# Half of the attention's q and k turned on VectorE and through memory instead of on TensorE

## The chip, the cores and the metric

The kernel runs on one core of one Trainium2 chip. Its time is device microseconds (us) for one execution. Five engines work side by side, each on its own queue of instructions: TensorE (PE) multiplies matrices into PSUM, VectorE (DVE) and ScalarE (ACT) do the element work, GpSimd (POOL) and SyncE (SP) mostly start transfers; ScalarE can start them too. They meet at semaphores.

## The reference

One layer of a bidirectional encoder, 512 tokens (8 rows of 64) by 1024 features:

```python
x = x + 0.5 * swiglu1(rmsnorm(x))
h = rmsnorm(x); xr, gr, q, k, v, ga, gb = split(h @ w_in)
y_lru = (rglru_fwd(conv(xr)) + rglru_bwd(conv(xr))) * gelu(gr)
q = rmsnorm_per_head(q, q_norm) * 64**-0.5;  k = rmsnorm_per_head(k, k_norm)
y_att = softmax(q k^T + relative_bias, 8 x 16 window) v      # 16 heads of 64
x = x + (sigmoid(ga) * y_lru + sigmoid(gb) * y_att) @ w_out
x = x + 0.5 * swiglu2(rmsnorm(x))
```

All is float32. A scale that only depends on the position within a head (`q_norm`, `k_norm`) sits on both sides of the product q k^T.

## The kernel before

Precise products are made from split operands: a weight tile `wraw` that was loaded by SP is cast to a rounded high part `wh` (line 138, ScalarE; in the gate chunks with odd f line 140, VectorE) and a low part `wl` = raw − high (line 141, VectorE), and each product is three matmuls (lines 166 to 168). There are four buffers each for `wh` and `wl` and three for `wraw`, used in turn: the cast for one chunk can begin when the matmuls that read the chunk four places before it have ended.

The stages follow each other on TensorE: FFN 1, the xr projection with the recurrent branch, the q, k and v projections for features 0 to 511 and then 512 to 1023 ("half 0" and "half 1", `hf`), then 24 gate chunks of 24 matmuls with 512 columns each (chunk 0 to 23 below: eight for `gr`, eight for `ga`, eight for `gb`), w_out and FFN 2. The work of the attention and of the recurrence is written as Python generators, `lanes`, from which `weave` takes a step at fixed rates (`RATE`) in the middle and at the end of each chunk; `hold` keeps an instruction behind the last chunk matmul recorded so far. From this the Tile framework's scheduler makes one fixed order for each engine.

`heads(hf)` is the attention of one half, in four groups `fi` of two heads. First q and k (tokens on the partitions, tiles `qk`) are multiplied by their norms `rq` (line 1004). Then, per group, `start(fi)` turns four 128 x 128 blocks of q and four of k on TensorE (lines 1013 and 1015, into PSUM), and splits them: `qh` and `kh` by ScalarE (1019, 1022), `ql` and `kl` by VectorE (1021, 1024). `scores(fi)` multiplies them (line 1045, the first matmul reads `kl` and `qh`), VectorE adds the bias table `bm` (1065), ScalarE takes the exponentials (1072, eight of them with an accumulator read each), VectorE scales the rows (1077). `ship` turns the weights in 32 x 32 blocks (1086, 1087), sends them to memory by SP and back by POOL as `PT`; `apply` (1108) multiplies with v, two groups later in half 1, and ScalarE copies the result out as `att` (1118). In half 1 `start(fi + 1)` follows `scores(fi)` in the program.

Between these, the gates are evicted by VectorE (1173), activated by ScalarE (1177) and multiplied into `A` (1187, 1190).

Of the kernel before, what the change touches and what calls it, by code (L numbers as in the profile page):

```python
# [16 lines left out]
P = 128  # L17
# [63 lines left out]
    "t1": {"att": 0.75, "tail": 0.75, "lru": 2},  # L81
    "g": {"att": 0.7, "tail": 0.7, "lru": 1.5, "v": 0.5},
# [4 lines left out]
def block_kernel(ctx: ExitStack, tc, a, out):  # L87
# [19 lines left out]
    NBIG = 42  # L107
# [553 lines left out]
    lanes = {"att": [], "tail": [], "lru": [], "v": []}  # L661
    due = {"att": 0.0, "tail": 0.0, "lru": 0.0, "v": 0.0}
# [113 lines left out]
    gk = small[:, C_KN : C_KN + 1]  # L776
# [27 lines left out]
    def lru():  # L804
# [52 lines left out]
        def use(f, d):  # L857
            r, ix = got[f, d]
            hold(nc.vector.tensor_tensor(ix, ix, xc[f], ALU.mult))
            th = big_t(n="th")  # L860
# [72 lines left out]
    def qk_raw(w, hf, st):  # L933
# [6 lines left out]
        for j, t in enumerate(raws):  # L940
            sq = big_t(n="sq")
# [41 lines left out]
    def bias(g):  # L983

        for hp in range(2):
            bms[g, hp] = tiny.tile([P, 640], F32, tag="bm", bufs=4, name=nm("bm"))
            ld = nc.gpsimd.dma_start(bms[g, hp], a["rpb"][g * 2 + hp])
            if g == 0:
                after(ld, mark["xr"])

    def heads(hf, raws, st):
# [9 lines left out]
        for w in range(2):  # L1001
            for j in range(NCB):
                t = raws[w][j].rearrange("p (h d) -> p h d", d=HD)
                hold(nc.vector.tensor_tensor(t, t, rq[:, w, j, :].unsqueeze(2).to_broadcast([P, 8, HD]), ALU.mult))
            yield
        qk, rss, soft, PTs = {}, {}, {}, {}


        def start(fi):
            fs = slice(fi * P, (fi + 1) * P)  # L1010
            pq, pk = aux_t(), aux_t()
            for j in range(NCB):
                hold(nc.tensor.transpose(pq[:, j * P : (j + 1) * P], raws[0][j][:, fs], ident))
            for j in range(NCB):
                hold(nc.tensor.transpose(perm(pk)[:, j], raws[1][j][:, fs], ident))
            rev = lambda t: t.rearrange("p (j t) -> p j t", j=NCB)[:, :, ::-1]
            fwd = lambda t: t.rearrange("p (j t) -> p j t", j=NCB)
            qh, ql, kh, kl = (big_t(F32R, n=n) for n in ("qh", "ql", "kh", "kl"))
            nc.scalar.activation(rev(qh), fwd(pq), AF.Copy, scale=gq8)
            with tc.high_priority():  # L1020
                nc.vector.scalar_tensor_tensor(rev(ql), fwd(pq), gq8, rev(qh.bitcast(F32)), ALU.mult, ALU.subtract)
            nc.scalar.activation(kh, pk, AF.Copy, scale=gk)
            with tc.high_priority():
                mark["kl"] = nc.vector.scalar_tensor_tensor(kl, pk, gk, kh.bitcast(F32), ALU.mult, ALU.subtract)
# [3 lines left out]
        def scores(fi, n2s):  # L1028
# [22 lines left out]
            for n2, hp in [(n2, hp) for n2 in n2s for hp in range(2)]:  # L1051
# [23 lines left out]
                for i, pt in enumerate(parts):  # L1075
                    n = n2 * 2 + i
                    nc.vector.tensor_scalar(pt, pt, rs[:, hp, n : n + 1], None, ALU.mult)
# [49 lines left out]
        if hf == 1:  # L1127
            yield
        LC = ATT_LAG[hf]
        for i, (fi, n2s) in enumerate(units):  # L1130
# [181 lines left out]
```

## Time and profile before

| what | value |
|---|---|
| median of 3 runs | 1084.0 us (1082.72 to 1085.13) |
| the profiled execution | 1082.5 us, span of its instructions 1080.7 us |
| busy: PE, DVE, ACT, POOL | 1075.3, 770.5, 561.6, 197.8 us |
| attention of half 0 (first turn, last scores) | 495 to 565 us of the span |
| attention of half 1 (first scores, last `apply`) | 598 to 675 us of the span |

The engines overlap, so their busy times don't add up; the span is what one engine's queue, with its waits, takes from the first instruction to the last. In a timeline each row is: start, duration, engine, line, operation, output <- inputs, count, and in brackets the idle time ahead of it and what ended that. In the groups of instructions the numbers are total busy time and mean duration in ns.

### The profile page before, as it was taken

To read this page: it belongs to the slowest core of one execution; us is meant where nothing else is said; L and a number is where in the kernel's file an instruction comes from. 1 tells how busy PE (TensorE), PEld (TensorE's weight loads), DVE (VectorE), ACT (ScalarE), POOL (GpSimd) and SP (SyncE) were. 2 spreads that over 40 slices of the span, in tenths; PEclk is the share of its full clock that TensorE was granted. 3 is DMA by queue.
4 is the path that set the end of the run, shared out by engine and by line. 5 is a ranking of instruction groups with operands and counts; after the bars stand their busy time and mean duration, and the time that the engine had idled before them with its cause. 6 is when DMAs were issued, how large, how long until landed. Compare 5 with 4: busy or idle time off the path is not lost.

```text
span 1080.7 us, 14413 instructions
## 1 busy us (share of the span) xinstructions
PE 1075.3 (99%) x5121; PEld 883.1 (82%) x5121; DVE 770.5 (71%) x1222; ACT 561.6 (52%) x867; POOL 197.8 (18%) x340
## 2 busy tenths in 40 slices
PE   9999999999999999999999999999999999999998
PEld 7888888888888778788877888888888888888887
DVE  7799778774327876999868986758687787764322
ACT  8755555553215778877354642456455555543320
POOL 0110002431000441330345232000001001332000
PEclk9999999999999999999999999999999999999999
DMA  9879675974324685573777576665476777676222
GB/s 356 182 228 246 180 192 135 248 250 148 98 83 146 194 231 155 169 212 104 229 235 219 170 242 205 192 223 160 97 188 188 187 210 167 184 241 198 93 71 79
DMA packets 67464, 198.18 MB, mean 183 GB/s; under 512 B 11072, under 2 KB 12864, under 8 KB 67392
## 3 DMA queue, kind: packets, MB, share of 16 engines
q1 hardware_dynamic: 46736, 136.66, 37.6%
q0 software_dynamic: 20512, 60.34, 25.0%
q8 instruction: 40, 0.66, 0.2%
q14 instruction: 32, 0.26, 0.1%
q10 hardware_dynamic: 144, 0.26, 0.1%
HBM read 162.06 MB, written 26.74 MB: 175 GB/s over the span
## 4 chain that ended last, share of the span: by engine, by line
PE 96%; DVE 2%; DMA 1%; ACT 1%; issue 0%; SPq 0%; ACTq 0%; DVEq 0%
PE acc L318 20%; PE aux L318 15%; PE acc L166 10%; PE acc L168 10%; PE acc L167 10%; PE acc L926 4%; PE acc L927 4%; PE acc L928 4%; PE aux L168 4%; PE aux L166 4%; PE aux L167 4%; PE aux L493 2%; PE aux L1108 1%; PE aux L837 1%; DMA vd<-v 1%; PE aux L1045 1%
## 5 line engine op out<-in xcount | busy, mean ns | idle before, releaser
L141 DVE TENSOR_TENSOR wl<-wraw,wh 128x1024 fp32r<-128x1024 f32 (+2 forms) x147 | 168.9, 1150 | 153.4 <-ACT wh L138 153.0
L138 ACT ACTIVATE wh<-wraw 128x1024 fp32r<-128x1024 f32 (+2 forms) x135 | 134.5, 998 | 224.6 <-PE acc L167 158.2
L141 DVE TENSOR_TENSOR wl<-pair,wh 128x1024 fp32r<-128x1024 f32 x80 | 97.6, 1223 | 42.2 <-ACT wh L138 41.9
L138 ACT ACTIVATE wh<-pair 128x1024 fp32r<-128x1024 f32 x80 | 84.7, 1061 | 77.5 <-PE aux L318 47.8
L166 PE MATMUL acc<-xh,wh 128*128 128x512 f32 x288 | 114.0, 396 | 0.0
L168 PE MATMUL acc<-xh,wl 128*128 128x512 f32 x288 | 112.6, 391 | 0.0
L167 PE MATMUL acc<-xl,wh 128*128 128x512 f32 x288 | 112.5, 391 | 0.0
L318 PE MATMUL aux<-wh,s 128*128 128x512 f32 x320 | 98.5, 389 | 0.0
L318 PE MATMUL acc<-wh,s 128*128 128x512 f32 x320 | 98.5, 389 | 0.0
L926 PE MATMUL acc<-wh,xh 128*128 128x512 f32 x192 | 75.7, 394 | 0.0
L927 PE MATMUL acc<-wh,xl 128*128 128x512 f32 x192 | 74.8, 389 | 0.0
L928 PE MATMUL acc<-wl,xh 128*128 128x512 f32 x192 | 74.7, 389 | 0.0
L318 PEld LDWEIGHTS acc<-wh,s 128*128 128x128 f32 x320 | 60.1, 188 | 12.5
L318 PEld LDWEIGHTS aux<-wh,s 128*128 128x128 f32 x320 | 60.1, 188 | 12.5
L167 PE MATMUL aux<-hl,wh 128*128 128x512 f32 (+1 forms) x179 | 69.3, 387 | 0.0
L168 PE MATMUL aux<-hh,wl 128*128 128x512 f32 (+1 forms) x179 | 69.3, 387 | 0.0
L166 PE MATMUL aux<-hh,wh 128*128 128x512 f32 (+1 forms) x179 | 69.0, 387 | 0.0
L168 PE MATMUL acc<-hh,wl 128*128 128x512 f32 (+1 forms) x176 | 68.1, 387 | 0.0
L167 PE MATMUL acc<-hl,wh 128*128 128x512 f32 (+1 forms) x176 | 68.1, 387 | 0.0
L166 PE MATMUL acc<-hh,wh 128*128 128x512 f32 (+1 forms) x176 | 68.0, 387 | 0.0
L166 PEld LDWEIGHTS acc<-xh,wh 128*128 128x128 f32 x288 | 54.1, 188 | 13.0 <-issue 2.3
L168 PEld LDWEIGHTS acc<-xh,wl 128*128 128x128 f32 x288 | 54.1, 188 | 11.5 <-issue 0.4
(230 smaller groups left out, 2412.3 us busy)
## 6 DMA issues: line engine op xcount, KB each, us to landing
wraw<-wqkv SPq DMA_DIRECT2D x24, 512.0 KB, 4.7
wraw<-wg SPq DMA_DIRECT2D x24, 512.0 KB, 8.0
wraw<-w1d SPq DMA_DIRECT2D x22, 512.0 KB, 3.7
wraw<-w2d SPq DMA_DIRECT2D x22, 512.0 KB, 3.4
PT<-w1s SPq DMA_DIRECT2D x20, 512.0 KB, 7.0
hT<-hd POOLq DMA_DIRECT2D x80, 128.0 KB, 3.9
PT<-w2s SPq DMA_DIRECT2D x20, 512.0 KB, 4.5
hd<-ht SPq DMA_DIRECT2D x32, 256.0 KB, 6.0
```

Source lines behind the costliest of these rows:

```text
L138: mark["H"] = nc.scalar.activation(H, raw, AF.Copy)
L141: mark["L"] = nc.vector.tensor_tensor(L, raw, H.bitcast(F32), ALU.subtract)
L166: nc.tensor.matmul(ps, wh, xh, start=first, stop=False, skip_group_check=skip)
L167: nc.tensor.matmul(ps, wh, xl, start=False, stop=False, skip_group_check=skip)
L168: mark["mm"] = nc.tensor.matmul(ps, wl, xh, start=False, stop=last, skip_group_check=skip)
L318: mark["mm"] = nc.tensor.matmul(pss[tb], x_[:, s], w_[:, c], start=first and k == 0 and x_ is xh_ and w_ is H, stop=k == 3 and w_ is L, sk ...
L493: mark["mm"] = nc.tensor.matmul(pre[tb], x_[:, tb * P : (tb + 1) * P], w_, start=k == 0 and x_ is xh[k] and w_ is H, stop=k == KT - 1 and ...
L837: prev, mm = mm, nc.tensor.matmul(ps[d][b], W[w][o, c], X[x][o], start=x == 1, stop=w + x == 0)
L926: nc.tensor.matmul(pss[j], xh[kk][:, tj], H[:, s], start=kk == 0, stop=False)
L927: nc.tensor.matmul(pss[j], xl[kk][:, tj], H[:, s], start=False, stop=False)
L928: mark["mm"] = nc.tensor.matmul(pss[j], xh[kk][:, tj], L[:, s], start=False, stop=kk == KT - 1)
L1045: mm = hold(nc.tensor.matmul(ps[hp][:, cs], q_[o, n * P : (n + 1) * P], keys(k_[o]), start=k_ is kl, stop=q_ is ql))
```

## The change

- For half 1 the 32 turns on TensorE go. After the norms, VectorE turns each pair of q and k tiles in 32 x 32 blocks (line 1013 of the new kernel) into a `pair` buffer, SP writes it to a new memory tile `qd` (1017, 1023), and `fetch(fi)` reads the blocks of one group back, turned, into `xqk`: four transfers started on ScalarE's queue (1033), 128 KB each, in pieces of 256 bytes. `qh`, `ql`, `kh`, `kl` are made from `xqk` in SBUF (1061 to 1066).
- There is one `xqk` buffer. `fetch(fi + 1)` stands behind the copies that read the group before.
- The norms and turns of half 1 are a lane of their own, `prep`, that runs while half 0's attention does; the first scores of half 1 come two chunks earlier.
- k's norm weight is multiplied into `gq8`, so k is only copied, and `kl` is a plain subtraction.
- In half 1 the rows of the softmax are scaled by ScalarE (1122) instead of VectorE.
- All gate weights are cast by ScalarE: twelve casts leave VectorE.
- The bias tables are loaded ahead of the scores that read the group before, at high priority.
- The pool of 2 KB tiles has 40 buffers instead of 42; the squares of q and k and three `tanh` tiles of the recurrence use other buffers.

```diff
     "t0": {"att": 0.0, "lru": 3.25},
-    "t1": {"att": 0.75, "tail": 0.75, "lru": 2},
-    "g": {"att": 0.7, "tail": 0.7, "lru": 1.5, "v": 0.5},
+    "t1": {"att": 0.75, "tail": 0.75, "lru": 2, "prep": 1.0},
+    "g": {"att": 0.7, "tail": 0.7, "lru": 1.5, "v": 0.5, "prep": 1.0},
 }
 ...
         return f"{s}_{uid[0]}"
-    NBIG = 42
+    NBIG = 40
     def big_t(dt=F32, shape=(P, T), n="b"):
 ...
     after(nc.vector.tensor_scalar(gq8, small[:, C_QN : C_QN + 1], HD**-0.5, None, ALU.mult), mark["h"])
-    gk = small[:, C_KN : C_KN + 1]
+    nc.vector.tensor_tensor(gq8, gq8, small[:, C_KN : C_KN + 1], ALU.mult)
     state = {}
 ...
             hold(nc.vector.tensor_tensor(ix, ix, xc[f], ALU.mult))
-            th = big_t(n="th")
+            if d == 1 and f < 3:
+                th = big.tile([P, T], F32, name=nm("th"), **(dict(tag="xqk", bufs=1) if f == 0 else dict(tag="PT", bufs=5)))
+            else:
+                th = big_t(n="th")
             act("tanh", nc.scalar.activation(th, r, AF.Tanh, scale=sp4[:, f * 2 + d : f * 2 + d + 1]))
 ...
         for j, t in enumerate(raws):
-            sq = big_t(n="sq")
+            sq = big.tile([P, T], F32, tag="pt", bufs=2, name=nm("sq"))
             after(nc.scalar.activation(sq, t, AF.Square), copy)
 ...
             bms[g, hp] = tiny.tile([P, 640], F32, tag="bm", bufs=4, name=nm("bm"))
-            ld = nc.gpsimd.dma_start(bms[g, hp], a["rpb"][g * 2 + hp])
+            with tc.high_priority():
+                ld = nc.gpsimd.dma_start(bms[g, hp], a["rpb"][g * 2 + hp])
             if g == 0:
                 after(ld, mark["xr"])
-    def heads(hf, raws, st):
+    def norm_qk(raws, st, qd):
         rq = tiny.tile([P, 2, NCB, 8], F32, tag="rq", name=nm("rq"))
 ...
         yield
-        for w in range(2):
-            for j in range(NCB):
+        out = []
+        for j in range(NCB):
+            for w in range(2):
                 t = raws[w][j].rearrange("p (h d) -> p h d", d=HD)
                 hold(nc.vector.tensor_tensor(t, t, rq[:, w, j, :].unsqueeze(2).to_broadcast([P, 8, HD]), ALU.mult))
+            if qd is not None:
+                t2 = pair_t().rearrange("p a b -> p (a b)")
+                for w in range(2):
+                    nc.vector.transpose(
+                        t2.rearrange("p (c f w i) -> p w f c i", c=NCB, f=4, w=2)[:, w],
+                        raws[w][j].rearrange("p (f c i) -> p f c i", c=NCB, i=32))
+                while out:
+                    hold(nc.sync.dma_start(*out.pop()))
+                out.append((qd[j], t2))
+                yield
+            elif j % 2 == 1:
+                yield
+        if qd is not None:
+            hold(nc.sync.dma_start(*out.pop()))
             yield
+            yield
+            fetch(qd, 0)
+
+    xs = {}
+
+    def fetch(qd, fi):
+        t = xs[fi] = big.tile([P, NCB * NCB, 2, 32], F32, tag="xqk", bufs=1, name=nm("xqk"))
+        for c in range(NCB):
+            hold(nc.scalar.dma_start(
+                t[c * 32 : (c + 1) * 32].rearrange("p g w i -> p g (w i)"),
+                qd.rearrange("j (a i) c f x -> c f i (j a) x", a=NCB)[c, fi]))
+
+    def heads(hf, raws, qd):
+
+        if hf == 1:
+            until("prep", lambda: False)
         qk, rss, soft, PTs = {}, {}, {}, {}
         def start(fi):
-            fs = slice(fi * P, (fi + 1) * P)
-            pq, pk = aux_t(), aux_t()
-            for j in range(NCB):
-                hold(nc.tensor.transpose(pq[:, j * P : (j + 1) * P], raws[0][j][:, fs], ident))
-            for j in range(NCB):
-                hold(nc.tensor.transpose(perm(pk)[:, j], raws[1][j][:, fs], ident))
             rev = lambda t: t.rearrange("p (j t) -> p j t", j=NCB)[:, :, ::-1]
-            fwd = lambda t: t.rearrange("p (j t) -> p j t", j=NCB)
+            if hf == 0:
+                fs = slice(fi * P, (fi + 1) * P)
+                pq, pk = aux_t(), aux_t()
+                for j in range(NCB):
+                    hold(nc.tensor.transpose(pq[:, j * P : (j + 1) * P], raws[0][j][:, fs], ident))
+                for j in range(NCB):
+                    hold(nc.tensor.transpose(perm(pk)[:, j], raws[1][j][:, fs], ident))
+                xq, xk = pq.rearrange("p (j t) -> p j t", j=NCB), pk
+                q_of, k_of = rev, lambda t: t
+            else:
+                x = xs.pop(fi).rearrange("p (j a) w i -> p w j a i", j=NCB)
+                xq, xk = x[:, 0], x[:, 1].rearrange("p j a (r c) -> p j a r c", r=2)
+                q_of = lambda t: rev(t).rearrange("p j (a i) -> p j a i", i=32)
+                k_of = lambda t: t.rearrange("p (a r j c) -> p j a r c", a=NCB, r=2, j=NCB)
             qh, ql, kh, kl = (big_t(F32R, n=n) for n in ("qh", "ql", "kh", "kl"))
-            nc.scalar.activation(rev(qh), fwd(pq), AF.Copy, scale=gq8)
+            hold(nc.scalar.activation(q_of(qh), xq, AF.Copy, scale=gq8))
             with tc.high_priority():
-                nc.vector.scalar_tensor_tensor(rev(ql), fwd(pq), gq8, rev(qh.bitcast(F32)), ALU.mult, ALU.subtract)
-            nc.scalar.activation(kh, pk, AF.Copy, scale=gk)
+                nc.vector.scalar_tensor_tensor(q_of(ql), xq, gq8, q_of(qh.bitcast(F32)), ALU.mult, ALU.subtract)
+            hold(nc.scalar.activation(k_of(kh), xk, AF.Copy))
             with tc.high_priority():
-                mark["kl"] = nc.vector.scalar_tensor_tensor(kl, pk, gk, kh.bitcast(F32), ALU.mult, ALU.subtract)
+                mark["kl"] = nc.vector.tensor_tensor(k_of(kl), xk, k_of(kh.bitcast(F32)), ALU.subtract)
             grid = lambda t: t.rearrange("p (r c) -> p r c", r=ROWS)
 ...
                     n = n2 * 2 + i
-                    nc.vector.tensor_scalar(pt, pt, rs[:, hp, n : n + 1], None, ALU.mult)
+                    if hf == 0:
+                        nc.vector.tensor_scalar(pt, pt, rs[:, hp, n : n + 1], None, ALU.mult)
+                    else:
+                        nc.scalar.activation(pt, pt, AF.Copy, scale=rs[:, hp, n : n + 1])
             return mm
 ...
         if hf == 1:
+            fetch(qd, 1)
             yield
         LC = ATT_LAG[hf]
         for i, (fi, n2s) in enumerate(units):
+            if 0 in n2s and hf * 4 + fi + 1 < KT:
+                bias(hf * 4 + fi + 1)
             behind = scores(fi, n2s)
 ...
                     start(fi + 1)
-                if hf * 4 + fi + 1 < KT:
-                    bias(hf * 4 + fi + 1)
             if phase[0] == "g":
                 yield
                 if hf == 1:
+                    if fi < 2:
+                        fetch(qd, fi + 2)
                     yield
 ...
         raws = [qk_raw(0, hf, st), qk_raw(1, hf, st)]
+        if hf == 1:
+            qd = dram.tile([NCB, P, NCB, 4, 64], F32, name="qd")
+            lanes["prep"].append(norm_qk(raws, st, qd))
         v_get(hf)
-        lanes["att"].append(heads(hf, raws, st))
+        if hf == 0:
+            lanes["att"].append(norm_qk(raws, st, None))
+        lanes["att"].append(heads(hf, raws, qd if hf == 1 else None))
         phase[0] = "t1" if hf == 0 else "g"
 ...
             ps = acc_t()
-            feat_chunk(a["wg3"][w * KT + f], KT, xh, xl, ps, 0, KT, f % 2 == 0, RATE[phase[0]])
+            feat_chunk(a["wg3"][w * KT + f], KT, xh, xl, ps, 0, KT, True, RATE[phase[0]])
             with tc.high_priority():
```

What the scheduler makes of it, at the places that matter below. **TensorE, at the first scores of half 1**: `acc` with `wh`, `wl` is a gate chunk, `kl`, `qh` belong to group 0. Before (end of chunk 8, then the scores):

```order
L166 MATMUL acc_5470<-xh_2741,wh_5472 128x512
L167 MATMUL acc_5470<-xl_2742,wh_5472 128x512
L168 MATMUL acc_5470<-xh_2741,wl_5473 128x512
L1045 MATMUL aux_5504<-kl_5421,qh_5418 128x256
L1045 MATMUL aux_5503<-kl_5421,qh_5418 128x256
L1045 MATMUL aux_5504<-kh_5420,qh_5418 128x256
L1045 MATMUL aux_5503<-kh_5420,qh_5418 128x256
```

Now (end of chunk 6, then the scores; chunk 7, with wh_5528, comes behind all 24 of them):

```order
L166 MATMUL acc_5390<-xh_2741,wh_5392 128x512
L167 MATMUL acc_5390<-xl_2742,wh_5392 128x512
L168 MATMUL acc_5390<-xh_2741,wl_5393 128x512
L1087 MATMUL aux_5415<-kl_5361,qh_5358 128x256
L1087 MATMUL aux_5414<-kl_5361,qh_5358 128x256
L1087 MATMUL aux_5415<-kh_5360,qh_5358 128x256
L1087 MATMUL aux_5414<-kh_5360,qh_5358 128x256
```

The scores stand directly behind a chunk's last matmul in both; now they stand two chunks earlier.

**ScalarE, the copies of group 0.** wh_5647 and wh_5849 are the casts of chunks 10 and 12. Before:

```order
L138 ACTIVATE wh_5647<-wraw_5646 128x1024
L1019 ACTIVATE qh_5418<-aux_5408,gq_2899 128x4x128
L1022 ACTIVATE kh_5420<-aux_5409,small 128x512
L1118 ACTIVATE att_5443<-aux_5426 128x512
L1177 ACT_TABLE_LOAD
L1177 ACTIVATE pair_5261<-pair_5261 128x1024
L138 ACTIVATE wh_5849<-wraw_5848 128x1024
```

Now, where wh_5766 is the cast of chunk 10 and wh_5937 that of chunk 11:

```order
L138 ACTIVATE wh_5766<-wraw_5765 128x1024
L1061 ACTIVATE qh_5358<-xqk_5103,gq_2899 128x4x128
L1064 ACTIVATE kh_5360<-xqk_5103 128x4x8x16
L1033 DMA xqk_5379<-qd 32x16x64 x4
L138 ACTIVATE wh_5937<-wraw_5936 128x1024
L1114 ACT_TABLE_LOAD
```

In both the copies stand behind the cast of chunk 10. That cast takes the buffer of chunk 6 (wh_5392 in TensorE's rows above), so what moved is the scores: from two chunks behind chunk 6 to directly behind it.

**VectorE, the same place.** Now, from the eviction of chunk 6 and the low part of chunk 10 to group 0's `kl`:

```order
L1226 TENSOR_TENSOR pair_5303<-acc_5390,rstd_2949 128x512
L141 TENSOR_TENSOR wl_5767<-wraw_5765,wh_5766 128x1024
L1120 TENSOR_SCALAR p_5238<-p_5238,rs_5131 128x256
L1120 TENSOR_SCALAR p_5237<-p_5237,rs_5131 128x192
L1132 STREAM_TRANSPOSE pt_5276<-p_5238 128x4x4x32
L1131 STREAM_TRANSPOSE pt_5276<-p_5237 128x3x4x32
L1240 TENSOR_TENSOR A_5296<-pair_4963,th_3385 128x512
L1240 TENSOR_TENSOR A_5298<-pair_4964,th_3514 128x512
L1240 TENSOR_TENSOR A_5300<-pair_4964,th_3594 128x512
L1063 SCALAR_TENSOR_TENSOR ql_5359<-xqk_5103,gq_2899,qh_5358 128x4x128
L1066 TENSOR_TENSOR kl_5361<-xqk_5103,kh_5360 128x4x8x16
```

Before, the same stretch held the norms and the copies (wl_5648 is chunk 10, wh_5809 chunk 11, acc_5389 chunk 7):

```order
L141 TENSOR_TENSOR wl_5648<-wraw_5646,wh_5647 128x1024
L1004 TENSOR_TENSOR qk_4312<-qk_4312,rq_5316 128x512
L1004 TENSOR_TENSOR qk_4314<-qk_4314,rq_5316 128x512
L1004 TENSOR_TENSOR qk_4316<-qk_4316,rq_5316 128x512
L1004 TENSOR_TENSOR qk_4318<-qk_4318,rq_5316 128x512
L1004 TENSOR_TENSOR qk_4555<-qk_4555,rq_5316 128x512
L1004 TENSOR_TENSOR qk_4557<-qk_4557,rq_5316 128x512
L1021 SCALAR_TENSOR_TENSOR ql_5419<-aux_5408,gq_2899,qh_5418 128x4x128
L1004 TENSOR_TENSOR qk_4559<-qk_4559,rq_5316 128x512
L1004 TENSOR_TENSOR qk_4561<-qk_4561,rq_5316 128x512
L140 CAST wh_5809<-wraw_5808 128x1024
L1173 TENSOR_TENSOR pair_5261<-acc_5389,rstd_2948 128x512
L1024 SCALAR_TENSOR_TENSOR kl_5421<-aux_5409,small,kh_5420 128x512
```

What stands between the low part of chunk 10 and `kl` are now scalings, block turns and gate products of other work; before it was the norms of q and k and an eviction.

**ScalarE, the copies of group 1.** Before (wh_5849 is chunk 12, which takes the buffer of chunk 8; the scores of group 1 stand behind chunk 10):

```order
L138 ACTIVATE wh_5849<-wraw_5848 128x1024
L1072 ACT_TABLE_LOAD
L1072 ACTIVATE p_5531,rs_5502<-so_5535,nmx_5536 128x192
L1072 ACTIVATE p_5532,rs_5502<-so_5535,nmx_5536 128x256
L1072 ACTIVATE p_5531,rs_5502<-so_5544,nmx_5545 128x3x64
L1072 ACTIVATE p_5532,rs_5502<-so_5544,nmx_5545 128x256
L1072 ACTIVATE p_5534,rs_5502<-so_5553,nmx_5554 128x256
L1072 ACTIVATE p_5533,rs_5502<-so_5553,nmx_5554 128x3x64
L1019 ACTIVATE qh_5601<-aux_5591,gq_2899 128x4x128
L1072 ACTIVATE p_5534,rs_5502<-so_5562,nmx_5563 128x256
L1072 ACTIVATE p_5533,rs_5502<-so_5562,nmx_5563 128x192
L1022 ACTIVATE kh_5603<-aux_5592,small 128x512
```

Now (wh_5977 is chunk 12; the scores of group 1 stand behind chunk 8):

```order
L138 ACTIVATE wh_5977<-wraw_5976 128x1024
L1122 ACTIVATE p_5442<-p_5442,rs_5413 128x192
L1122 ACTIVATE p_5443<-p_5443,rs_5413 128x256
L1122 ACTIVATE p_5442<-p_5442,rs_5413 128x192
L1122 ACTIVATE p_5443<-p_5443,rs_5413 128x256
L1114 ACTIVATE p_5444,rs_5413<-so_5464,nmx_5465 128x3x64
L1061 ACTIVATE qh_5502<-xqk_5379,gq_2899 128x4x128
L1114 ACTIVATE p_5445,rs_5413<-so_5473,nmx_5474 128x256
L1122 ACTIVATE p_5445<-p_5445,rs_5413 128x256
L1122 ACTIVATE p_5444<-p_5444,rs_5413 128x192
L1114 ACTIVATE p_5444,rs_5413<-so_5473,nmx_5474 128x192
L1064 ACTIVATE kh_5504<-xqk_5379 128x4x8x16
```

The two copies stand behind the cast of chunk 12 in both. The scores moved from behind chunk 10 to behind chunk 8, the chunk whose buffer that cast takes. The groups after it repeat this: group 2's copies stand behind the cast of chunk 14, its scores directly behind chunk 10; group 3's behind the cast of chunk 16, its scores behind chunk 12.

More of the change, by code (lines that the diff above doesn't have):

```diff
@@ L658, in ffn @@
         end(t1, o)
-    lanes = {"att": [], "tail": [], "lru": [], "v": []}
-    due = {"att": 0.0, "tail": 0.0, "lru": 0.0, "v": 0.0}
+    lanes = {"att": [], "tail": [], "lru": [], "v": [], "prep": []}
+    due = {"att": 0.0, "tail": 0.0, "lru": 0.0, "v": 0.0, "prep": 0.0}
     def weave(rate):
```

## The prediction

> **What bounds the kernel now.** I read the page's busy shares, then the chain that ended last, then the windows of the stage that the change touches, then single instructions there.
>
> ```profile
> span 1080.7 us, 14413 instructions
> PE 1075.3 (99%) x5121; PEld 883.1 (82%) x5121; DVE 770.5 (71%) x1222; ACT 561.6 (52%) x867; POOL 197.8 (18%) x340
> ...
> PE 96%; DVE 2%; DMA 1%; ACT 1%; issue 0%; SPq 0%; ACTq 0%; DVEq 0%
> ```
>
> TensorE is busy in 1075.3 of 1080.7 us and the chain runs along it. So every instruction taken from TensorE counts in full, and so does every new wait in its queue. In the stage of half 1's attention the windows show nothing else near that:
>
> ```profile
> core 0: us, PE busy (x) PEld busy (x) DVE busy (x) ACT busy (x) POOL busy (x), PEclk, DMA share, GB/s
> 600.00:620.00 20.00, 20.00 (x136) 16.60 (x136) 17.74 (x64) 11.77 (x36) 5.92 (x11) 1.00 0.56 182
> 620.00:640.00 20.00, 20.00 (x134) 16.73 (x133) 19.63 (x57) 9.02 (x27) 5.11 (x11) 1.00 0.76 232
> 640.00:660.00 20.00, 20.00 (x129) 16.62 (x128) 16.74 (x44) 8.54 (x21) 6.50 (x12) 1.00 0.64 196
> ```
>
> TensorE has no gap in these 60 us, VectorE is busy for 54.1 and ScalarE for 29.3. The change moves work to ScalarE, where there is room on average. What matters is where in its queue the copies of q and k stand.
>
> **Term 1, removed: 32 turns.** The place of one group of eight, on TensorE:
>
> ```profile
> 613.59 0.39 PE L168 MATMUL acc<-xh,wl 128*128 128x512 f32 x1
> 613.91 0.39 PE L1045 MATMUL aux<-kl,qh 64*128 64x256 f32 x2
> ...
> 615.58 0.66 PE L1013 MATMUL aux<-ident,qk 128*128 128x128 f32 x4
> 616.08 0.60 PE L1015 MATMUL aux<-ident,qk 128*128 128x128 f32 x4
> 616.43 0.48 PE L166 MATMUL acc<-xh,wh 128*128 128x512 f32 x1
> ...
> L1013 PE MATMUL aux<-ident,qk 128*128 128x128 f32 x32 | 5.7, 287 | 0.0
> L1015 PE MATMUL aux<-ident,qk 128*128 128x128 f32 x32 | 5.4, 277 | 0.0
> ```
>
> From the first turn to the next chunk's matmul pass 0.85 us, so four groups are 3.4 us; half of the two lines' busy time is 5.55 us (group 0's turns are interleaved and cost more). I take 4.5 us off the path.
>
> **Term 2, the waits that the new order makes.** A weight cast waits for the chunk whose buffer it takes:
>
> ```profile
> 613.79 1.06 ACT L138 ACTIVATE wh<-wraw 128x1024 fp32r<-128x1024 f32 x1 [2.05 <-PE acc L167]
> ...
> 616.42 0.46 ACT L1072 ACTIVATE p<-so,nmx 128x192 f32<-128x192 f32 x1 [1.57 <-DVE nmx L1065]
> ...
> 619.23 0.67 ACT L1019 ACTIVATE qh<-aux,gq 128x512 fp32r<-128x512 f32 x1
> 619.80 0.50 ACT L1072 ACTIVATE p<-so,nmx 128x256 f32<-128x256 f32 x1
> ...
> 620.73 0.67 ACT L1022 ACTIVATE kh<-aux,small 128x512 fp32r<-128x512 f32 x1
> ```
>
> This is the cast of chunk 14, which waited for the last matmul on chunk 10's high part and began 0.12 us before the scores (613.79 against 613.91) that stand behind chunk 10. Those scores read copies made long before: the next group's copies, at 619.23 and 620.73, are for scores that TensorE reaches a chunk pair later. In the new order the scores of group 0, 1, 2, 3 stand directly behind chunks 6, 8, 10, 12, and their copies behind the casts of chunks 10, 12, 14, 16, which wait for exactly those chunks. The engines work their queues in order, so TensorE reaches the scores and waits for all that stands on ScalarE or VectorE from that cast to `kl`, however early the data was fetched. Nothing hides it: the next chunk's matmuls stand behind the scores. The prices:
>
> ```profile
> L138 ACT ACTIVATE wh<-wraw 128x1024 fp32r<-128x1024 f32 x120 | 127.1, 1059 | 222.8 <-PE acc L167 157.6 <-issue 29.2 <-PE acc L927 18.0
> L141 DVE TENSOR_TENSOR wl<-wraw,wh 128x1024 fp32r<-128x1024 f32 x132 | 161.0, 1220 | 153.4 <-ACT wh L138 153.0
> L1077 DVE TENSOR_SCALAR p<-p,rs 128x256 f32<-128x256 f32 x32 | 11.4, 355 | 0.1
> L1077 DVE TENSOR_SCALAR p<-p,rs 128x192 f32<-128x192 f32 x32 | 10.3, 322 | 0.1
> L1087 DVE STREAM_TRANSPOSE pt<-p 128x512 f32<-128x512 f32 x16 | 11.0, 689 | 0.0
> L1086 DVE STREAM_TRANSPOSE pt<-p 128x384 f32<-128x384 f32 x16 | 8.9, 553 | 0.0
> L1187 DVE TENSOR_TENSOR A<-pair,th 128x512 f32<-128x512 f32 x8 | 5.1, 674 | 0.0
> L1021 DVE SCALAR_TENSOR_TENSOR ql<-aux,gq,qh 128x512 fp32r<-128x512 f32 x8 | 5.9, 741 | 3.6 <-ACT qh L1019 3.6
> L1004 DVE TENSOR_TENSOR qk<-qk,rq 128x512 f32<-128x512 f32 x16 | 10.1, 686 | 0.0
> L1072 ACT ACT_TABLE_LOAD x4 | 5.1, 1283 | 2.3 <-DVE nmx L1065 2.2
> L138 ACT ACTIVATE hh<-hT 128x256 fp32r<-128x256 f32 x80 | 26.7, 402 | 0.0
> L1118 ACT ACTIVATE att<-aux 128x512 f32<-128x512 f32 x8 | 4.7, 584 | 6.1 <-PE aux L1108 6.1
> ```
>
> An exponential with its read takes 0.47 us in a row of them (616.42 to 619.23 holds six), `qh` 0.57 (619.23 to 619.80), `kh` 0.67, the new `kl` 0.69 as the subtraction of the same size in line 1004. A row scaling on ScalarE is not in the trace; the nearest is its copy of 256 columns, 0.33 us in a row (26.7 over 80); for 192 columns it is less, at the least 0.25 (three quarters). I take 0.33.
>
> - Group 0, by VectorE: cast 1.06, low part 1.22, two scalings 0.68, two block turns 1.24, three gate products 2.02, `ql` 0.74, `kl` 0.69, together 7.65; less 0.12, and 0.4 for the overlap of eight neighbours (the 16 of line 1004 take 10.1 us at 686 ns each, 0.05 us less apiece): 7.1 us. By ScalarE alone it would be 1.06 + 0.57 + 0.67 + 0.69 − 0.12 = 2.9 us, the lower end.
> - Group 1, by ScalarE: cast 1.06, six scalings 2.0, three exponentials 1.4, `qh` 0.57, `kh` 0.67, `kl` 0.69: 6.4 − 0.12 = 6.3 us.
> - Group 2: the same with a table load, 1.28, and eight exponentials, 3.8, in place of three: 10.1 − 0.12 = 9.9 us.
> - Group 3: cast, eight scalings 2.6, three exponentials 1.4, an `att` copy 0.58, two copies 1.24, `kl` 0.69: 7.6 − 0.12 = 7.5 us.
>
> Sum: 30.8 us. The lower end, with 2.9 in group 0 and scalings of 192 columns at 0.25: about 26 less 1, 25 us. The upper end adds 1 us a group, since VectorE was busy for 54.1 of 60 us and an exponential can wait for its bias sum: 35 us.
>
> **What costs nothing, and its cover.** The twelve casts that go to ScalarE (12 x 1.06), 32 scalings (32 x 0.33) and 16 issues make some 30 us more of ScalarE over the some 130 us of the gate chunks (24 of 24 matmuls at 0.23 us), where it was about half idle; weights are cast up to three chunks ahead (some 16 us), which covers a queue that runs a few us late. An issue on ScalarE has one row, 0.41 us:
>
> ```profile
> L476 ACTq DMA_DIRECT2D wraw<-w1gu x1: 408/408/408, 0.7 to 0.7; - x1
> ...
> hT<-hd POOLq DMA_DIRECT2D x80, 128.0 KB, 3.9
> gate<-pair POOLq DMA_DIRECT2D x64, 128.0 KB, 5.1
> ```
>
> A `fetch` is four transfers of 128 KB; such ones land in 3.9 to 5.1 us. Each is issued behind the `kl` of the group before and has two chunks, over 10 us, until its copy; so it is hidden, and SP's four writes of `qd` too, which end three chunks before the first copy. VectorE gives up 12 casts and 32 scalings and gains eight block turns of 0.69: some 14 us less, off the path. Forty buffers instead of 42 leave the order in both FFNs as it was; the price there is nothing unless a tile is still held, which no row shows. The earlier bias loads only lengthen POOL's queue, 18% busy. A later end of the attention would matter only behind chunk 23; its last `apply` now stands in chunk 17.
>
> **The sum.** 1080.7 − 4.5 + 30.8 = 1107.0 us of span. The profiled execution took 1082.5 (1.8 more than its span), the runs' median is 1.5 above that: 1110 us. Own range 1080.7 − 5.5 + 25 + 3.3 = 1103 to 1080.7 − 3.4 + 35 + 3.3 = 1116.
>
> **Rivals.**
>
> - *TensorE starts slowly behind each wait.* In the trace its first matmuls, after the idle start, are slow:
>
> ```profile
> L132 PE MATMUL aux<-ones 128*128 128x128 f32 x16 | 3.8, 431 | 1.1 <-DVE pol L762 1.1
> L220 PE MATMUL aux<-ident,ssum 128*128 128x128 f32 x8 | 1.3, 279 | 0.0
> ```
>
>   431 ns against 279 for the same shape: of 3.8 us 1.3 are lost. Four such starts make 5.3 us, 1115. Against it: the granted clock reads 1.00 in every window, and no later idle time is over 0.5 us, so the trace has no second start to read. [...]
> - *Faster: the waits don't arise.* If ScalarE's queue reaches the copies before TensorE ends the chunk, only term 1 is left: 1084.0 − 4.5 = 1079.5. It decides at `kl` of each group ending before chunks 6, 8, 10 and 12 do. For it: before, the copies were always in time. Against it: the cast ahead of them can't begin before that chunk's last read, as the row at 613.79 shows.
> - *Only one of the four waits stands*, by some 5 us, and cancels the gain: 1084.
> - *The fetch is late too.* If 256-byte pieces take four times the 5.1 us, groups 1 to 3 wait some 8 us more each: 1134. For it, only that these pieces are half as long as those of `hT`.
>
> **How the numbers follow.** The forecast has 0.66 (1110), the slow restarts 0.18 (1115), the late fetch 0.04, the faster case 0.09, one wait 0.03. The range of 8 in 10 reaches from 1099, a little under the own range for cases with two or three of the waits whole, to 1119, which takes in most of the restarts. A change of under 0.2% (2.2 us) can't be told from none here. Slower by more: 0.66 + 0.18 + 0.04 = 0.88; within: 0.03; faster: 0.09.
>
> **What would show it.** In the new profile TensorE should wait four times for `kl` (line 1066) at its first `scores` matmul (1087), by some 7, 6, 10 and 7 us, the first near 583 us of the span, the others 15 to 30 us apart; the cast of line 138 should begin with each wait. TensorE's busy time should fall by 4 to 5 us and its idle time rise by about 30. Idle time of ScalarE ahead of `qh`, released by `xqk`, would show a late fetch; matmuls of 512 columns at a wider spacing than 0.23 us behind the waits would show slow restarts. If TensorE goes through the four places without a gap, the forecast is wrong in term 2.

## The result, and the profile after

The changed kernel takes 1118.25 us (median of 6 runs, 1117.71 to 1120.12) against 1083.72 us (6 runs, 1082.26 to 1085.13): 1.0322 times as long, 95% interval 1.0308 to 1.0335. The prediction said 1110, with a range of 1099 to 1119. The profiled execution took 1117.7 us. Its page, the lines that answer to those shown of before:

```profile
span 1115.8 us, 14411 instructions
PE 1078.8 (97%) x5089; PEld 887.4 (80%) x5089; DVE 760.3 (68%) x1187; ACT 585.3 (52%) x911; POOL 197.5 (18%) x340
...
PEclk9999999999999999999998889999999999999999
...
PE 94%; DVE 3%; ACT 2%; issue 1%; DMA 1%; SPq 0%; ACTq 0%; DVEq 0%
```

TensorE stands idle for 1115.8 − 1078.8 = 37.0 us, where it was 5.4: 31.6 us more. Its busy time rose by 3.5 us although it has 32 instructions fewer, and in three slices of the clock row the granted clock is below full speed. Both point to the stage of half 1's attention. The waits of TensorE (what waited for what: us in total, times, longest), and the windows of that stage (columns as in the prediction):

```profile
PE aux L1087 <- DVE kl L1066: 32.0, 4, 10.2
PE aux L132 <- DVE pol L762: 1.1, 1, 1.1
```

```profile
580.00:620.00 40.00, 26.38 (x157) 21.58 (x156) 22.30 (x57) 17.79 (x40) 17.67 (x29) 0.83 0.71 208
620.00:660.00 40.00, 27.40 (x174) 22.52 (x172) 19.65 (x54) 22.01 (x51) 7.00 (x13) 0.87 0.48 131
660.00:700.00 40.00, 34.21 (x230) 28.65 (x231) 20.02 (x49) 18.91 (x47) 9.68 (x17) 0.91 0.61 193
```

Four waits for `kl` hold 32.0 us; no other wait is over 1.1 us. No engine is near full in these windows: this is a chain, not a load. One of the four in the timeline, group 1, behind chunk 8:

```profile
606.95 0.39 PE L168 MATMUL acc<-xh,wl 128*128 128x512 f32 x1
607.15 1.06 ACT L138 ACTIVATE wh<-wraw 128x1024 fp32r<-128x1024 f32 x1 [0.60 <-PE acc L167]
...
608.11 1.58 ACT L1122 ACTIVATE p<-p,rs 128x192 f32<-128x192 f32 x4
...
609.60 0.44 ACT L1114 ACTIVATE p<-so,nmx 128x192 f32<-128x192 f32 x1
...
610.04 0.71 ACT L1061 ACTIVATE qh<-xqk,gq 128x512 fp32r<-128x512 f32 x1
...
611.14 0.84 ACT L1122 ACTIVATE p<-p,rs 128x256 f32<-128x256 f32 x2
...
611.89 0.44 ACT L1114 ACTIVATE p<-so,nmx 128x192 f32<-128x192 f32 x1
...
612.33 0.61 ACT L1064 ACTIVATE kh<-xqk 128x512 fp32r<-128x512 f32 x1
...
612.97 0.69 DVE L1066 TENSOR_TENSOR kl<-xqk,kh 128x512 fp32r<-128x512 f32 x1 [0.35 <-ACT kh L1064]
...
613.72 0.58 PE L1087 MATMUL aux<-kl,qh 64*128 64x256 f32 x2 [6.38 <-DVE kl L1066]
...
616.24 0.41 PE L1087 MATMUL acc<-kh,ql 64*128 64x256 f32 x2
616.58 0.79 PE L166 MATMUL acc<-xh,wh 128*128 128x512 f32 x1
617.17 0.63 PE L167 MATMUL acc<-xl,wh 128*128 128x512 f32 x1
617.60 0.63 PE L168 MATMUL acc<-xh,wl 128*128 128x512 f32 x1
618.02 0.47 PE L166 MATMUL acc<-xh,wh 128*128 128x512 f32 x1
618.33 0.39 PE L167 MATMUL acc<-xl,wh 128*128 128x512 f32 x1
```

Two things are to be seen. First, the cast of line 138 begins as the chunk's last matmuls end, and from there ScalarE's queue runs without a gap to `kh` (scalings, exponentials, two copies), then VectorE to `kl`: 6.38 us. Second, TensorE comes back slow. The 24 scores matmuls take 2.86 us (613.72 to 616.58), where those of before took 1.67 (613.91 to 615.58 in the prediction's rows), and the next matmuls of 512 columns stand 0.43 us apart in place of 0.227 until 618.02.

In group 0 it is VectorE's queue that holds `kl`, as forecast: `kh` was done at 585.99, and the low part of the cast, scalings, block turns, three gate products and `ql` stand between.

```profile
585.38 0.61 ACT L1064 ACTIVATE kh<-xqk 128x512 fp32r<-128x512 f32 x1
...
587.79 1.85 DVE L1240 TENSOR_TENSOR A<-pair,th 128x512 f32<-128x512 f32 x3
...
590.22 0.68 DVE L1066 TENSOR_TENSOR kl<-xqk,kh 128x512 fp32r<-128x512 f32 x1
```

The same reading for all four groups; "lost" is the time from the first scores matmul to the first matmul at full pace again, less what the same rows take in the kernel before:

| group | wait forecast | wait measured | 24 scores | lost to slow matmuls |
|---|---|---|---|---|
| 0 | 7.1 | 7.24 | 2.86 | 1.2 + 0.2 |
| 1 | 6.3 | 6.38 | 2.86 | 1.2 + 0.7 |
| 2 | 9.9 | 10.24 | 2.86 | 1.2 + 0.8 |
| 3 | 7.5 | 8.14 | 2.86 | 1.2 + 0.3 |
| sum | 30.8 | 32.0 | | 6.8 |

So the span grew by 35.1 us = 32.0 of waits + 6.8 of slow matmuls − 3.7, and 3.7 us is what is left for the turns that went. The busy time agrees to a few tenths: 6.8 − 3.7 = 3.1 us more by this, 3.5 measured. The theory to test has three parts: the waits come from the order of the queues, the slow matmuls from the waits, and nothing else in the change costs anything. "Before" is 1083.2 to 1083.6 us beside each run below.

### The profile page after: what moved, and what is told of

Its sections match the earlier page's. It is cut to its first block, busy times and chain, and to the rows that moved or that the text cites. A ratio compares the mean times of both kernels' runs of the same rounds, so it can differ in the third digit from the quotient of the medians.

```text
span 1115.8 us, 14411 instructions
## 1 busy us (share of the span) xinstructions
PE 1078.8 (97%) x5089; PEld 887.4 (80%) x5089; DVE 760.3 (68%) x1187; ACT 585.3 (52%) x911; POOL 197.5 (18%) x340
## 4 chain that ended last, share of the span: by engine, by line
PE 94%; DVE 3%; ACT 2%; issue 1%; DMA 1%; SPq 0%; ACTq 0%; DVEq 0%
PE acc L318 19%; PE aux L318 15%; PE acc L166 10%; PE acc L167 10%; PE acc L168 10%; PE acc L929 4%; PE acc L930 4%; PE acc L931 4%; PE aux L167 4%; PE aux L168 4%; PE aux L166 4%; PE aux L493 2%; PE aux L1153 1%; PE aux L1087 1%; PE aux L837 1%
## 5 line engine op out<-in xcount | busy, mean ns | idle before, releaser
L138 ACT ACTIVATE wh<-wraw 128x1024 fp32r<-128x1024 f32 (+2 forms) x147 | 147.2, 1003 | 285.3 <-PE acc L167 210.3
```

What stands on the lines that cost most here:

```text
L138: mark["H"] = nc.scalar.activation(H, raw, AF.Copy)
```

## Experiments: is the slow clock a result of the waits?

Matmuls whose product is overwritten fill the idle time ahead of the scores. In `fill1`:

```diff
+            for _ in range((28, 24, 40, 32)[fi] if hf == 1 else 0):
+                hold(nc.tensor.matmul(pss[n2s[0]][0], xh[1][:, :P], xh[0], start=True, stop=True))
             for n in [n2 * 2 + i for n2 in n2s for i in range(2)]:
```

> The changed kernel with 28, 24, 40 and 32 extra matmuls of 512 columns (their product is overwritten) in TensorE's queue just ahead of the first scores of groups 0 to 3 of half 1, where TensorE idled for 7.24, 6.38, 10.24 and 8.14 us. At 0.227 us each they fill all but some 1 us of each wait. Theory: the loss has two parts, the waits (32.0 us) and slow matmuls behind them (6.8 us, from the spacing of the rows behind each wait against the same rows of the kernel before), and the second comes from the idle time. Then 124 more matmuls make the kernel faster: 1118.3 - 6.8 = 1111.5 us, up to 1114 where the fillers outlast a wait; the scores behind a wait take 1.7 us a group, not 2.86. Rival: the slow matmuls have nothing to do with idling (they come from the copies in SBUF or from the transfers): 1118 us or more, and the scores still take 2.86 us.

`fill3` has 19, 15, 32 and 23 of them:

> The same with fewer extra matmuls, 19, 15, 32 and 23, which leave some 3 us of idle time ahead of the scores of each group in place of 7.24, 6.38, 10.24 and 8.14. Theory as it stands: the slow stretch needs a long idle time, and with 3 us it is weaker or gone: 1111.5 to 1114 us. Rival: any gap of some us brings the same slow stretch, about 1.7 us a group: 1118 us. Between them the spacing of the scores matmuls decides: 1.7 us for the 24 of a group when fast, 2.86 when slow.

Then, with the result of these two known, `fill_all` with 27, 52, 44 and 36:

> The changed kernel with 27, 52, 44 and 36 extra matmuls ahead of the scores of the four groups, 159 in all or 36.0 us at 0.227: enough to leave no idle time of over 1 us, where the 124 of the first such run left 2.3 to 2.7 us in three groups. Theory: with no idle time there is no slow clock in any execution, and the time is the changed kernel's, less 6.8 us of slow matmuls, plus the 36.0 - 32.0 = 4.0 us by which the fillers outlast the waits: 1118.3 - 6.8 + 4.0 = 1115.5 us (1114 to 1116.5), with a granted clock of 1.000 throughout. Rival: the slow clock does not come from idle time, and the fillers only add their 4 us: 1122 us and a mean clock of 0.986 as in the changed kernel.

Measured: `fill1` 1117.32 us (ratio to before 1.0316, 1.0299 to 1.0334), `fill3` 1116.62 (1.0310, 1.0295 to 1.0325), `fill_all` 1115.35 (1.0295, 1.0281 to 1.0309). In group 0 the scheduler put the added matmuls eight to twelve chunk matmuls ahead of the scores. The waits of `fill1` and, below, one restart in `fill3`:

```profile
PE aux L1089 <- DVE kl L1066: 7.5, 3, 2.7
```

```profile
639.31 0.39 PE L1089 MATMUL aux<-kl,qh 64*128 64x256 f32 x2 [3.01 <-DVE kl L1066]
...
641.07 0.69 PE L1155 MATMUL aux<-PT,va 128*64 128x128 f32 x4
...
641.98 1.92 PE L1155 MATMUL aux<-PT,vs 128*64 128x128 f32 x16
...
644.11 0.48 PE L1155 MATMUL aux<-PT,ve 128*64 128x128 f32 x4
644.52 0.50 PE L166 MATMUL acc<-xh,wh 128*128 128x512 f32 x1
```

`fill_all` settles it. Its windows, to be set against the three of the changed kernel above:

```profile
580.00:620.00 40.00, 38.41 (x225) 31.42 (x224) 22.91 (x59) 21.69 (x43) 16.98 (x27) 1.00 0.64 188
620.00:660.00 40.00, 40.00 (x239) 33.02 (x240) 18.55 (x57) 18.94 (x51) 7.70 (x14) 1.00 0.50 145
660.00:700.00 40.00, 40.00 (x263) 32.95 (x262) 20.18 (x45) 18.83 (x43) 9.65 (x17) 1.00 0.66 202
```

With 159 more matmuls the kernel is 2.9 us faster than the changed one (ratio to before 1.0295 against 1.0322), the clock reads 1.00 in all three windows, and the four score blocks take 1.67 to 1.69 us. 1118.3 − 6.8 + 4.0 = 1115.5 was expected. The traces close the sum too: a gap of 1.6 us was left, so waits and fillers are 37.6 us, 5.6 more than the waits of the changed kernel; 5.6 − 6.8 = −1.2, and the span is 1.4 us shorter (1114.4). So the 6.8 us come from idle time and go with it.

`fill1` was expected at 1111.5 to 1114, which only its profiled execution all but met (1114.13 us, clock 1.000, all blocks at 1.67 to 1.71). Two reasons. The added matmuls moved some of ScalarE's and VectorE's work in the order, so that waits and fillers together were 7.5 + 28.1 = 35.6 us where the wait had been 32.0. And in its three other executions, of which there is no trace, the mean clock was 0.995 to 0.997 and the time 2.8 to 3.6 us longer: the same program slowed in these three and not in the one whose gaps were 2.3 to 2.7 us; what gaps the three had is not shown. `fill3`, expected in the same range, missed it by over 2 us and shows both, slow and fast, in one trace: behind 1.50 us of idle time the scores took 1.68 us; behind 3.01 they ran at full speed (1.76) and the slow stretch came late, on the `apply` in the rows above, 3.45 us in place of 1.90; behind 4.37 and 4.50 they took 2.86.

## Experiments: is it the order of the queues?

`later` moves the scores to where they stood before and leaves all else:

```diff
             fetch(qd, 1)
             yield
+            yield
+            yield
+            yield
```

> The changed kernel with three more empty steps ahead of the first scores of half 1, so that the four scores stand behind chunks 8, 10, 12 and 15, as in the kernel before. Nothing else is changed. The copies of group 0 now stand behind the cast of chunk 10, two chunks ahead of their scores; those of groups 1 and 2 behind the casts of chunks 14 and 16, which wait for chunks 10 and 12, just ahead of their scores; those of group 3 behind the cast of chunk 19, which waits for chunk 15. Theory: what costs is a copy behind a cast that waits for the chunk ahead of the scores, so only group 0's wait goes (7.2 us and 1.4 us of slow matmuls) and the three others stay, at 5 to 9 us each: 1104 to 1110 us. Rival: the scores simply came two chunks too early for the data, and at the old places no wait is left: about 1080 us.

Measured: 1103.89 us, ratio 1.0194 (1.0179 to 1.0209).

```profile
PE aux L1087 <- DVE kl L1066: 19.9, 3, 7.9
```

Group 0's wait is gone, three are left (7.89, 7.36 and 4.62 us; the last, and the time, are a little under the range given), each followed by a block of 2.86 us. The forecast by the casts holds to the group; that the scores were "simply too early" does not.

`copies_first` keeps the scores and moves the casts of gate weights behind copies emitted three chunks earlier:

```diff
             split(raw[:, s], H[:, s], L[:, s], act)
+        if act and behind_kh[0] is not None:
+            after(mark["H"], behind_kh[0])
 ...
-            hold(nc.scalar.activation(k_of(kh), xk, AF.Copy))
+            mark["kh"] = hold(nc.scalar.activation(k_of(kh), xk, AF.Copy))
 ...
+            khs.append(mark.get("kh"))
+            behind_kh[0] = khs[-3] if len(khs) >= 3 else None
             feat_chunk(a["wg3"][w * KT + f], KT, xh, xl, ps, 0, KT, True, RATE[phase[0]])
```

> The changed kernel with one order added on ScalarE: the cast of a gate chunk stands behind every copy kh that was emitted three chunks or more ahead of it. The copies of group 0 then stand behind the cast of chunk 7 in place of 10, those of groups 1, 2 and 3 behind the casts of chunks 8, 10 and 12 in place of 12, 14 and 16. Theory: group 0's copies are then clear of the chunk ahead of the scores, so its wait (7.24 us and 1.4 us of slow matmuls) goes. In the other groups the copies still have eight exponentials and six to eight scalings of the group before ahead of them, and those exponentials wait for scores that end two chunks earlier, so these waits stay in part: 5 to 11 us each, 1105 to 1112 us in all. Rival: the casts alone are to blame, and with the copies ahead of them all four waits go: 1080 to 1085 us.

Measured: 1106.69 us, ratio 1.0220 (1.0206 to 1.0234); waits of 0, 5.76, 11.20 and 6.55 us. Group 0's went, as it should when the cast is its only gate. What holds the others is in the timeline of group 2, behind chunk 10:

```profile
620.46 0.69 DVE L1232 TENSOR_TENSOR pair<-acc,rstd 128x512 f32<-128x512 f32 x1 [6.87 <-PE acc L171]
...
622.27 0.35 DVE L1110 CUSTOM_DVE_ANT_0 so<-aux,bm 128x192 f32<-128x192 f32 x1
...
622.66 0.46 ACT L1117 ACTIVATE p<-so,nmx 128x192 f32<-128x192 f32 x1 [6.67 <-DVE nmx L1110]
...
630.13 0.62 ACT L1067 ACTIVATE kh<-xqk 128x512 fp32r<-128x512 f32 x1
...
631.62 0.58 PE L1090 MATMUL aux<-kl,qh 64*128 64x256 f32 x2 [11.20 <-DVE kl L1069]
```

There is a second gate of the same kind, on VectorE: the eviction of the gate chunk (line 1226 of the changed kernel, 1232 here) waits for the chunk ahead of the scores and stands ahead of the bias sums of the group before; their exponentials stand ahead of the copies on ScalarE. The prediction counted those exponentials, but named only the cast as what starts the chain.

`scale_dve` takes the row scaling out of the chain:

```diff
-                    if hf == 0:
-                        nc.vector.tensor_scalar(pt, pt, rs[:, hp, n : n + 1], None, ALU.mult)
-                    else:
-                        nc.scalar.activation(pt, pt, AF.Copy, scale=rs[:, hp, n : n + 1])
+                    nc.vector.tensor_scalar(pt, pt, rs[:, hp, n : n + 1], None, ALU.mult)
```

> The changed kernel with the row scaling of the softmax of half 1 back on VectorE (32 instructions). In the changed kernel's trace 6, 7 and 8 such scalings stand on ScalarE between the cast and kh of groups 1, 2 and 3, 0.37 us each: 2.2, 2.6 and 3.0 us of those waits. Theory: the waits are the sum of what stands between the cast and kl, so these three shrink by that, less what the scalings cost in VectorE's queue when they stand ahead of kl there (0.3 us each, up to half of it): 4 to 8 us, 1110 to 1114 us; group 0's 7.24 stays. Rival: ScalarE's work is not what the scores wait for (they wait for VectorE or for the fetch): 1118 us or slower, since VectorE gets 10.8 us more work.

Measured: 1108.24 us, ratio 1.0229 (1.0214 to 1.0244), some 2 us better than the range given.

```profile
PE aux L1087 <- DVE kl L1066: 23.1, 4, 7.2
```

The waits are 7.22, 4.29, 7.24 and 4.38 us: group 0 as before, the others 2.1, 3.0 and 3.8 us shorter. The scalings had taken 2.2, 2.2 and 3.0 us on ScalarE there (six of them in group 2, not seven). The rest is other work that changed its place: in group 2 a table load (1.3 us) and an exponential left the stretch and a gate activation (0.95) came in; in group 3 an exponential and the `att` copy left it. On VectorE the scalings cost little: `kl` began 0.2 us behind the end of `kh` in groups 1 and 2, and 0.6 in group 3, where block turns had held it for 0.5 before. The rival (it is not ScalarE's work that is waited for) falls.

## Experiments: the terms that were small

`turns2` does the 32 turns of half 1 twice in the kernel before:

```diff
-                hold(nc.tensor.transpose(pq[:, j * P : (j + 1) * P], raws[0][j][:, fs], ident))
+                for _ in range(1 + hf):
+                    hold(nc.tensor.transpose(pq[:, j * P : (j + 1) * P], raws[0][j][:, fs], ident))
```

(and likewise for k).

> The kernel before with the 32 turns of half 1 done twice (the second writes the same values to the same place). It prices the first term by itself: 32 turns more. By the prediction's rows 0.85 us for eight, 3.4 us in all, at the least, and 5.55 us by the busy time of their lines at the most; the difference of the two traces leaves 3.7 us. So 1087.1 to 1089.3 us, most likely 1087.5. Rival: the turns stood beside something that TensorE waited for anyway, so that they cost less than 2 us: under 1085.7 us.

Measured: 1086.48 us against 1083.16, ratio 1.0034 (1.0021 to 1.0046): 3.3 us by the medians, just under the 3.4 that were expected at the least.

`act_both` puts the row scaling of half 1 and all gate casts on ScalarE in the kernel before (the edit of the scaling is that of the change):

```diff
-            feat_chunk(a["wg3"][w * KT + f], KT, xh, xl, ps, 0, KT, f % 2 == 0, RATE[phase[0]])
+            feat_chunk(a["wg3"][w * KT + f], KT, xh, xl, ps, 0, KT, True, RATE[phase[0]])
```

> The kernel before with two of the change's edits alone: the row scaling of half 1 on ScalarE and all gate weights cast by ScalarE. They were priced at nothing. Theory: the copies of q and k stand where they stood, with scores two chunks behind, so some 25 us more on ScalarE and 22 us less on VectorE change nothing: 1082 to 1086 us. Rival: ScalarE is too full in the gate chunks with this work, and its queue makes TensorE wait by itself, whatever the place of the copies: over 1090 us.

Measured: 1082.91 us, ratio 0.9996 (0.9987 to 1.0005). The page's busy line has the work moved and TensorE as full as ever:

```profile
span 1081.4 us, 14420 instructions
PE 1076.0 (99%) x5121; PEld 884.5 (82%) x5121; DVE 756.0 (70%) x1178; ACT 584.8 (54%) x910; POOL 197.7 (18%) x340
```

So the same 32 scalings are free where the copies have two chunks to spare, and make some 7.4 us of the waits where they stand between the gate and `kl`.

## Experiments: a version without the waits

`all_moved` takes the copies out of the way of both gates. It has the order of `copies_first`, with four chunks for three, the scaling of `scale_dve`, and

```diff
-    "g": {"att": 0.7, "tail": 0.7, "lru": 1.5, "v": 0.5, "prep": 1.0},
+    "g": {"att": 0.65, "tail": 0.65, "lru": 1.5, "v": 0.5, "prep": 1.0},
 ...
             fetch(qd, 1)
             yield
+            yield
+            yield
+            yield
+            yield
 ...
+            if hf == 1 and fi < 3:
+                start(fi + 1)
             behind = scores(fi, n2s)
 ...
-            if 0 in n2s:
+            if 0 in n2s and hf == 0:
                 if fi < 3:
                     start(fi + 1)
```

> The changed kernel with the q and k copies taken out of the way of both things that stood ahead of them: a cast stands behind the copies that were emitted four chunks ahead; the copies of the next group are emitted ahead of the scores of this one, in place of behind them; the row scaling of half 1 is VectorE's again; four empty steps more ahead of the first scores, and a rate of 0.65 in place of 0.70 steps for the attention, put the scores behind chunks 9, about 11, 14 and 16. Theory: the turns through memory save 3.7 us of TensorE (what is left of the difference when waits and slow matmuls are taken off), and with no wait over 2.5 us left that saving shows: waits of 0 to 4 us in all, 1080 to 1084 us, against 1083.7 before. Rival: with the copies ahead of them the casts come late, and TensorE waits for its weights in place of kl: over 1090 us.

Measured: 1082.59 us, ratio 1.0000 (0.9991 to 1.0008). All four waits for `kl` are gone and no cast is late, but a new wait stands behind the scores of group 3:

```profile
652.51 0.46 PE L1153 MATMUL aux<-PT,va 128*64 128x128 f32 x4 [1.89 <-DVE nmx L1110]
...
654.18 0.80 PE L169 MATMUL acc<-xh,wh 128*128 128x512 f32 x1
654.77 0.63 PE L170 MATMUL acc<-xl,wh 128*128 128x512 f32 x1
655.20 0.63 PE L171 MATMUL acc<-xh,wl 128*128 128x512 f32 x1
655.62 0.63 PE L169 MATMUL acc<-xh,wh 128*128 128x512 f32 x1
```

`apply` needs a tile that a late bias sum still reads; here matmuls 0.43 us apart followed a gap of 1.89 us. Two kernels shift the places a little. `moved_b` has a rate of 0.64 and three steps:

> The first rearranged kernel (copies ahead of scores, casts behind the copies of four chunks ago, scaling on VectorE) with a rate of 0.64 in place of 0.65 and three empty steps in place of four. In that kernel one wait of 1.89 us stood behind the scores of group 3, for a bias sum that frees an aux tile, and 1.6 us of slow matmuls behind it: 3.5 us that ate the 3.3 us which the removed turns are worth. The new places shift the scores of groups 1 to 3 by half a chunk against the chunk pairs. Theory: if that wait goes, 1079.5 to 1081.5 us, faster than before (1083.2) by 0.2 to 0.3%. Rival: the softmax of half 1 is too tight for VectorE at any such place, another wait of 1 to 3 us takes over: 1082 to 1086 us.

`moved_c` has a rate of 0.64, five steps and three chunks:

> As the run before, with a rate of 0.64, five empty steps, and casts behind the copies of three chunks ago: the scores stand behind chunks 10, 12, 15 and 17. Theory: the later places leave VectorE more of the gate chunks, the wait behind the scores of group 3 goes, 1079.5 to 1081.5 us. Rival: later attention comes late for the last gates (its last apply now stands some two chunks later), so that TensorE waits for the split of y ahead of w_out: 1082 to 1086 us.

Measured: `moved_b` 1079.27 us, ratio 0.9964 (0.9952 to 0.9977); `moved_c` 1079.20, ratio 0.9962 (0.9949 to 0.9976). Both beat both kernels. The page's first lines and the longest wait of TensorE in `moved_b`:

```profile
span 1077.4 us, 14410 instructions
PE 1072.4 (100%) x5089; PEld 880.5 (82%) x5089; DVE 765.4 (71%) x1219; ACT 570.7 (53%) x877; POOL 197.1 (18%) x340
```

```profile
PE aux L132 <- DVE pol L765: 1.1, 1, 1.1
```

The longest is the one at the program's start that all the kernels have (1.1 us); none is left in the stage (`moved_c` keeps one of 0.8 us, with no slow matmuls behind it), and the span is 3.3 us under the 1080.7 of before, what `turns2` gave for the turns. By the medians the gain is 4.3 us (interval 2.5 to 5.2); that the last us has another source is possible and not shown.

## Why the prediction was right, and where it was wrong

- **Direction and mechanism: right.** Four waits for `kl` at the first `scores` matmul; the first began at 590.95 − 7.24 = 583.7 us (forecast near 583), the others began 23 to 27 us apart, and the cast of line 138 began within 0.2 us of each.
- **Term 2: right, 32.0 for 30.8 us.** Each wait came through the engine that was named for it, VectorE in group 0 and ScalarE in the others. The two largest misses are groups 2 and 3 (+0.3, +0.6). A row scaling on ScalarE was taken at 0.33 us and takes 0.37 (in the rows of group 1, four of 192 columns go from 608.11 to 609.60 and two of 256 from 611.14 to 611.89): most of the miss in group 2. In group 3 a shorter `att` copy and cast make up for half of that, and `kl` stood 0.5 us behind the end of `kh`, held by two block turns on VectorE, which that group's sum did not have:

```profile
663.86 0.61 ACT L1064 ACTIVATE kh<-xqk 128x512 fp32r<-128x512 f32 x1
663.91 0.70 DVE L1132 STREAM_TRANSPOSE pt<-p 128x512 f32<-128x512 f32 x1
664.54 0.54 DVE L1131 STREAM_TRANSPOSE pt<-p 128x384 f32<-128x384 f32 x1
665.00 0.65 DVE L1066 TENSOR_TENSOR kl<-xqk,kh 128x512 fp32r<-128x512 f32 x1
```

- **Term 1: too large, 4.5 for 3.3 to 3.7 us.** The spacing of the rows, 0.85 us for eight turns, gave 3.4, and was right. The durations of the turns overlap (0.66 + 0.60 us in 0.85 us of path), so the busy time of their lines should not have pulled the number up.
- **The step that failed is the rival of the slow restarts, kept out of the sum and given 0.18.** It came true, with the forecast's waits. From the forecast span of 1107.0 the way to 1115.8 is 6.8 of slow matmuls + 1.2 of longer waits + 0.8 of cheaper turns. The time outside the span was 2.45 us for 3.3 forecast. So 1118.25 lies above the own range (to 1116) and inside the wide one (to 1119), which had been stretched for these restarts. What was held against the rival, a clock of 1.00 in every window and no second start to read, was no evidence: TensorE of the kernel before never waited for over 1.1 us, where the four waits are 6.38 to 10.24, so its trace held no start like theirs. The one row with a start in it, line 132, spoke for it. Its size, 1.3 us a start, came out at 1.7 in the mean: 6.8 us in the sum, 1.4 to 2.0 for the single waits.
- **What costs nothing: right.** `act_both` has the ratio 0.9996, and no wait of TensorE but the four is over 1.1 us, which covers the 40 buffers, the bias loads and the writes of `qd`. The fetch was never late: `qh` never waited for it.

```profile
L1061 ACT ACTIVATE qh<-xqk,gq 128x512 fp32r<-128x512 f32 x4 | 2.8, 707 | 0.0
L1033 ACTq DMA_DIRECT2D xqk<-qd x16: 309/509/1490, 568.4 to 642.3; - x16
```

  An issue on ScalarE's queue took 0.51 us at the median and up to 1.49 (the second row: shortest, median, longest in ns), where one row of before gave 0.41.
- **TensorE's busy time** was to fall by 4 to 5 us and rose by 3.5: slow matmuls count as busy. The idle time rose by 31.6 (forecast some 30).

## What to carry to other kernels

When work moves from the bounding engine to engines with room, don't count their room; find in each in-order queue the instruction that waits for the bounding engine (here a weight cast and a chunk's eviction) and see on which side of it the moved work lands. Then price every long wait of TensorE twice, by its length and by the slow matmuls behind it (here 1.4 to 2.0 us behind each of 6.38 to 10.24), and look for a start from idle in the trace to size the second (here 1.3 us, for 1.7 measured). A saving of 0.3% shows only when the last such wait is gone: three orders of nearly the same work gave 1118, 1083 and 1079 us.

## What the runs showed of the hardware that was not expected

The prediction had slow starts only as a rival; the runs give their onset, in the profiled executions. Behind gaps of 1.50, 1.59, 2.33, 2.47 and 2.68 us the 24 scores took 1.67 to 1.71 us; behind 4.29 to 4.38 they took 2.49 to 2.86, and behind every one of 4.50 to 11.20 us 2.86. At 3.01 us the slow stretch began 1.8 us after the gap, and one gap of 1.89 us, between scores and `apply` in `all_moved`, was followed by one too. So the length of the gap alone does not tell here: 2.68 us in `fill1` had no slow matmuls behind it, 1.89 in `all_moved` had. Nor did a longer gap cost more: 10.24 us of idle lost 2.0 us, 6.38 us lost 1.9. The slow matmuls of 512 columns stood 0.43 us apart in place of 0.227, nearly half speed.
